# Gate and up products of a SwiGLU feed-forward with still weights: three 256 wide matmuls become one of 512 and one of 256, and their halves are added when they are read

## The chip, the cores and the metric

The kernel runs on one core of a Trainium2 chip. The metric is the device time of one execution in microseconds. The kernel before takes 1019.05 us in the median of 3 runs (1018.81 to 1019.17).

## The reference

A decoder trunk of two layers over 256 tokens with model width 1024, all in float32. Every layer has a feed-forward (FFN), a token mixer (a gated recurrence in layer 1, attention in layer 2) and a second FFN, each with normalisation before and after. The change lies in the FFN, which runs four times with a hidden width of 2816:

```python
def swiglu(x, w_gate, w_up, w_down):
    return (jax.nn.silu(x @ w_gate) * (x @ w_up)) @ w_down
```

## The kernel before

**Number format.** A float32 product is made of three matmuls: every operand `a` is split into a rounded upper part `hi` and a lower part `lo = a - hi`, and `hi*hi + hi*lo + lo*hi` is summed in PSUM. The normalised input of an FFN lies transposed in one tile `xall` of [128 rows of the model width, 8 such slices `k`, 2 parts, 256 tokens], so that for each slice the upper part's 256 columns and the lower part's 256 columns stand side by side; `xhi` and `xlo` are views of it.

**Weights.** A unit is 128 x 1024 weights (512 KB). SyncE loads it into one of 5 `raw` buffers (`load_raw`, L160); ScalarE copies it to `whi` (`split`, L175) and VectorE subtracts to get `wlo` (L176). There are 9 pairs of `whi` and `wlo`, so a unit can be split up to 9 units before it is used; the split of unit i waits until unit i - 9 is used up.

**Order of the work.** TensorE's order is written out by hand: a list of items, each of which prepares one unit (`prep`) and uses it (`work`). `slot` (L359) does one item; `tick` (L84) after it starts the next split and lets deferred small work run (`defer(n, fn)` runs `fn` n ticks later). The order on ScalarE, VectorE and GpSimd is set by the framework's scheduler, and each of these engines works its list strictly in order.

**An FFN** (`ffn_items`, L479, and `run_ffn`, L606). The hidden width is cut into five tiles of 512 and one of 256.
- In three of the four FFNs tile 0 is computed with the inputs as stationary operand and the weights moving (`proj_items`, `mm3`, L183 to L185); its hidden rows are then transposed (`hidden_T`, L506).
- All other tiles keep the weights still: a 128 x 128 block of weights is the stationary operand, and the inputs of all 256 tokens move past it (`mmj`, L195). Each call issues three matmuls of 256 columns: `whi` with `xhi` (L198), `whi` with `xlo` (L199), `wlo` with `xhi` (L200), all into the same 256 columns. I call 32 calls of `mmj` (8 slices `k` by 4 blocks of weights) a *block*: each tile of 512 is a gate block and then an up block (`tile_items`, L535); the tile of 256 is one block with gate and up in halves (`last_items`, L558). There are 38 blocks, 9 in each of three FFNs and 11 in the one where all tiles are of this kind: 1216 calls. The blocks of an FFN are counted from 1: in the first FFN, block 1 is gate and block 2 up of tile 1, block 3 and 4 those of tile 2, and so on.
- A block accumulates in two banks of PSUM, two products of 256 columns in each. When it ends, `gate_rows` (L518) runs for each bank: VectorE multiplies by the tokens' norms (L521), ScalarE takes the silu (L523). `up_rows` (L525) multiplies up by gate on VectorE (L528), and splits the product into `hhi` (ScalarE, L532) and `hlo` (VectorE, L533), the operands of the down projection.
- The down projection is `row_items` (L440): hidden rows stationary, weights moving, 512 columns per matmul, `mm3` again.

**PSUM** has 8 banks of 512 columns: 4 named `mm` for accumulation, 2 named `gt` and 2 named `tr` for transposes and other small products (L62 to L69). Each name is a ring; the framework makes a writer wait until the bank's former readers are done.

**Small work inside the blocks.** In the first FFN, `rg_params` (L670) transposes the parameters of the recurrence on TensorE (L672) some 40 ticks in, into a `tr` bank.

Of the kernel before, what the change touches and what calls it, by code (L numbers as in the profile page):

```python
# [9 lines left out]
F32 = mybir.dt.float32  # L10
# [34 lines left out]
def trunk_kernel(ctx: ExitStack, tc: tile.TileContext, A: dict, out: bass.AP):  # L45
# [15 lines left out]

    def mmbank():  # L62
        return psum.tile([P, 512], F32, tag="mm", name=nm("mm"), bufs=4)

    def gtbank():
        return psum.tile([P, 512], F32, tag="gt", name=nm("gt"), bufs=2)

    def trbank():
        return psum.tile([P, 512], F32, tag="tr", name=nm("tr"), bufs=2)  # L69
# [125 lines left out]
    def mmj(ps, wh, wl, k, first, last):  # L195

        tensor_work(3 * S)
        nc.tensor.matmul(ps, wh, xhi[:, k, :], start=first, stop=False)  # L198
        nc.tensor.matmul(ps, wh, xlo[:, k, :], start=False, stop=False)  # L199
        nc.tensor.matmul(ps, wl, xhi[:, k, :], start=False, stop=last)  # L200
# [55 lines left out]
    def rstd_rows():  # L256

        tp = trbank()
# [124 lines left out]
    def proj_items(w, c0, nn, get_x, post, nk=8):  # L383
# [4 lines left out]
        for k0 in range(0, nk, kper):  # L388
# [8 lines left out]
            def work(t, u, k0=k0, kn=kn, i=len(items)):  # L397
                if k0 == 0:
                    acc[t] = mmbank()
                ps = acc[t][:, :nn]  # L400
                if i < 2:
                    for m in range(3):
                        for j in range(kn):
                            nc.tensor.matmul(ps, get_x(t, k0 + j)[m == 2], [u.hi, u.lo, u.hi][m][:, j * nn:(j + 1) * nn],
                                             start=k0 + j + m == 0, stop=False)
                    return
                for j in range(kn):
                    k = k0 + j
                    mm3(ps, *get_x(t, k), u.hi[:, j * nn:(j + 1) * nn], u.lo[:, j * nn:(j + 1) * nn], k == 0, k == nk - 1)
                if k0 + kn == nk:  # L410
                    post(t, acc[t][:, :nn])
            if not items:
# [27 lines left out]
    def row_items(w, widths, get_x, post, rows=2):  # L440
# [6 lines left out]
        for k, kp in enumerate(widths):  # L447
# [3 lines left out]
            def work(t, u, k=k):  # L451
# [13 lines left out]
                if k == nk - 1:  # L465
                    post(t, acc[t])
            items.append((prep, work))
# [11 lines left out]
    def ffn_items(pool_of, wg, wu, wd, post_g, next_dests, last=False, normed=False, lead=1):  # L479
# [10 lines left out]
        def gate_tile():  # L490
            return pool_of().tile([P, 512], F32, tag="sil", name=nm("sil"), bufs=2)

        def prod_tile():
            return pool_of().tile([P, 8 * HA], F32, tag="prod", name=nm("prod"), bufs=2)[:, :512]

        def post_gate(t, ps):
            s = sil[t] = gate_tile()
            nc.scalar.activation(s, ps, AF.Silu, scale=rs[t][:, 0:1])

        def post_up(c0):  # L500
            def f(t, ps):
                pr = prod_tile()
# [3 lines left out]
            def hidden_T(pr, t):  # L506
                hh, hl = hid_tiles()
                tp = trbank()
# [9 lines left out]
        def gate_rows(n, ps):  # L518
            s = sil["j", n] = gate_tile()
            v = s.rearrange("p (a b) -> p a b", a=2)  # L520
            nc.vector.tensor_tensor(v, ps.rearrange("p (a b) -> p a b", a=2),  # L521
                                    rcp["v"].unsqueeze(1).to_broadcast([P, 2, S]), ALU.mult)
            nc.scalar.activation(s, s, AF.Silu)  # L523

        def up_rows(n, ps, k0):  # L525
            hh, hl = hid_tiles()
            pr = prod_tile()
            nc.vector.tensor_tensor(pr, ps, sil["j", n], ALU.mult)  # L528
            pv = pr.rearrange("p (a t b) -> p a t b", a=2, t=2)
            hv = hh[:, :, k0:k0 + 2, :].rearrange("p t a b -> p a t b")  # L530
            lv = hl[:, :, k0:k0 + 2, :].rearrange("p t a b -> p a t b")
# [3 lines left out]
        def tile_items(w, c0, post):  # L535
            acc = {}

            for k0 in range(0, 8, 2):
# [4 lines left out]
                def work(t, u, k0=k0):  # L543
                    if k0 == 0:
                        acc["b"] = [mmbank(), mmbank()]
                    for j in range(2):
                        for b in range(4):
                            o = j * 512 + b * P
                            mmj(acc["b"][b // 2][:, (b % 2) * S:(b % 2 + 1) * S], u.hi[:, o:o + P], u.lo[:, o:o + P],
                                k0 + j, k0 + j + b % 2 == 0, k0 + j == 7 and b % 2 == 1)  # L550
                        if j == 0:
                            tick()
                    if k0 == 6:
                        for n in range(2):
                            post(n, acc["b"][n])
                items.append((prep, work))

        def last_items(c0):  # L558
            acc = {}

            for k0 in range(0, 8, 2):
# [7 lines left out]
                def work(t, u, k0=k0):  # L569
                    if k0 == 0:  # L570
                        acc["b"] = [mmbank(), mmbank()]
                    for j in range(2):
                        for b in range(4):
                            o = j * 512 + b * P
                            mmj(acc["b"][b // 2][:, (b % 2) * S:(b % 2 + 1) * S], u.hi[:, o:o + P], u.lo[:, o:o + P],
                                k0 + j, k0 + j + b % 2 == 0, k0 + j == 7 and b % 2 == 1)
                        if j == 0:
                            tick()
                    if k0 == 6:
                        gate_rows(0, acc["b"][0])  # L580
                        up_rows(0, acc["b"][1], c0 // P)
# [3 lines left out]
        for i in range(5):  # L585
# [84 lines left out]
    def rg_params():  # L670
        tp = trbank()
# [34 lines left out]
    def add_gate_unit(g, k0, kn):  # L706
# [5 lines left out]
        def work(t, u):  # L712
# [6 lines left out]
            if k0 + kn == 8:  # L719
                if (g, t) not in ((0, 1), (2, 0)):  # L720
                    for gg, tt_ in {(1, 1): [(0, 1)], (2, 1): [(2, 0)]}.get((g, t), []) + [(g, t)]:
                        n = GCOLS[gg][1]
                        tok = toks[(gg, tt_)] = pools["r"].tile([P, 4 * RT], F32, tag="tok", name=nm("tok"), bufs=4)
                        nc.scalar.activation(tok[:, :n], gacc[(gg, tt_)][:, :n], AF.Gelu_apprx_tanh)
        rg[f"g{sum(n[0] == 'g' and n[1] != 'w' for n in rg)}"] = len(items)
# [36 lines left out]
    def conv(p, ps):  # L762
# [9 lines left out]
        def taps(j, i):  # L772
            for k in (2, 1, 0):
                s = 3 - k
                nc.vector.scalar_tensor_tensor(xc[:w, j, s:], ps[:w, j * S:(j + 1) * S - s],
                                               par[:w, k * NRT + i:k * NRT + i + 1], xc[:w, j, s:], ALU.mult, ALU.add)

# [80 lines left out]
    def batch(g):  # L858
# [20 lines left out]
        def gate_T(t):  # L879
            tok = toks[(g, t)]  # L880
            tp = tps[t] = trbank()
# [4 lines left out]
        def product(t):  # L886
# [4 lines left out]
            for (a, b, w) in parts_of(g):  # L891
                tp = tps[t][:w, a * P:b * P].rearrange("p (a b) -> p a b", a=b - a)
                nc.vector.tensor_tensor(y[:w, a:b, :], tp, tt[g][:w, a:b, t * P:(t + 1) * P], ALU.mult)
                nc.scalar.activation(yy[g][0][:w, t, a:b, :], y[:w, a:b, :], AF.Copy)

# [83 lines left out]
    def heads_T(pool, ps, t, n, scale, cols, dst):  # L979

        tok = pool.tile([P, 8, HA], F32, tag="prod", name=nm("htok"), bufs=2)
# [8 lines left out]
        def turn(b):  # L990
            tp = trbank()
# [42 lines left out]
    def v_items(c0, n, extra):  # L1034
# [3 lines left out]
        for k0 in range(0, 8, 2):  # L1038
# [9 lines left out]
            def work(t, u, k0=k0):  # L1048
# [6 lines left out]
                if k0 == 6:  # L1055
                    if extra:
                        post_f(t, ps[:, n:])
                    nc.scalar.activation(kv["v"][t][:, c0:c0 + n], ps[:, :n], AF.Copy, scale=rs[t][:, 0:1])
            items.append((prep, work))
# [21 lines left out]
    def attention(t):  # L1081
# [32 lines left out]
        def values(hg):  # L1114
# [8 lines left out]
            if hds[-1] % 8 == 7:  # L1123
# [3 lines left out]
                                        sm.unsqueeze(2).to_broadcast([P, 8, HD]), ALU.mult)  # L1127

# [199 lines left out]
```

## Time and profile before

| | |
|---|---|
| median of 3 runs | 1019.05 us |
| the profiled execution | 1018.94 us |
| its span, first to last instruction | 1017.2 us |
| granted TensorE clock over the span | 0.998 |
| calls of `mmj`, matmuls in them | 1216, 3648 of 6518 |
| moved by DMA | 179.07 MB, mean 176 GB/s |
| stretches in which `mmj` runs | 35.8 to 140.4, 340.0 to 444.2, 555.4 to 683.1, 846.4 to 950.6 us |

How to read it: in the profile PE is TensorE's matmuls, PEld its loads of the stationary operand, DVE is VectorE, ACT ScalarE, POOL GpSimd, SP SyncE (DMA issue). A row of a group gives the line, the engine, the operation, output and inputs by their names, the count, the busy time in us, the mean duration of one in ns, and after the second bar the engine's idle time before these instructions with what ended it. A row of the timeline gives the start and the duration in us and then the same. Matmuls are pipelined: the next one starts before the last one's row ends.

### The profile page before, as it was taken

How to read it: one execution, taken by the hardware profiler on the slowest of the kernel's cores; microseconds unless marked ns; L12 is line 12 of the kernel's file. 1: busy time of each engine (PE TensorE's matmuls, PEld its weight loads, DVE VectorE, ACT ScalarE, POOL GpSimd, SP SyncE). 2: the span in 40 equal slices, each digit the busy share in tenths (PEclk: the TensorE clock that was granted, in tenths of full speed). 3: DMA queues.
4: the chain of work that ended last, by engine and by line, in shares of the span. 5: the costliest groups of instructions: out<-in, count | busy, mean ns of one | idle time of the engine just before them, and what ended most of it. 6: DMA issues, size and time to landing. Idle time of an engine off the chain costs nothing.

```text
span 1017.2 us, 16436 instructions
## 1 busy us (share of the span) xinstructions
PE 1004.2 (99%) x6518; PEld 915.0 (90%) x6518; DVE 628.3 (62%) x777; ACT 533.9 (52%) x734; POOL 52.7 (5%) x113
## 2 busy tenths in 40 slices
PE   8999999999999999999999999999999999999997
PEld 5999998889988999998898999998888889999885
DVE  5866554668997655554695555654477476556442
ACT  5645434559986544443565444443467565444331
POOL 2500000000003000000110000000020010000000
PEclk9999999999999999999999999999999999999999
DMA  6886646565336766556376666664555067665441
GB/s 231 284 257 198 192 160 187 164 183 151 122 99 226 229 186 186 187 151 180 116 242 221 191 181 180 185 183 164 165 167 166 1 189 247 186 183 182 155 125 41
DMA packets 91875, 179.07 MB, mean 176 GB/s; under 512 B 11790, under 2 KB 31318, under 8 KB 91798
## 3 DMA queue, kind: packets, MB, share of 16 engines
q1 hardware_dynamic: 90550, 176.89, 56.1%
q8 instruction: 51, 0.84, 0.3%
q10 hardware_dynamic: 608, 1.06, 0.3%
q0 software_dynamic: 640, 0.07, 0.1%
q14 instruction: 26, 0.21, 0.1%
HBM read 176.95 MB, written 1.05 MB: 175 GB/s over the span
## 4 chain that ended last, share of the span: by engine, by line
PE 90%; ACT 4%; DVE 4%; issue 2%; POOL 1%; DVEq 0%; POOLq 0%; ACTq 0%
PE mm L198 14%; PE mm L200 14%; PE mm L199 14%; PE mm L185 13%; PE mm L184 13%; PE mm L183 13%; PE gt L815 1%; DVE wlo L176 1%; PE mm L190 1%; PE mm L191 1%; PE mm L192 1%; PE gt L1094 1%; PE mm L1121 1%; ACT junk L213 1%; PE gt L222 1%
## 5 line engine op out<-in xcount | busy, mean ns | idle before, releaser
L176 DVE TENSOR_TENSOR wlo<-raw,whi 128x1024 fp32r<-128x1024 f32 (+4 forms) x329 | 395.1, 1207 | 297.2 <-ACT whi L175 295.4
L175 ACT ACTIVATE whi<-raw 128x1024 fp32r<-128x1024 f32 (+4 forms) x329 | 342.6, 1046 | 373.8 <-PE mm L199 207.9
L198 PE MATMUL mm<-xall,whi 128*128 128x256 f32 x1216 | 344.7, 283 | 0.0
L200 PE MATMUL mm<-xall,wlo 128*128 128x256 f32 x1216 | 344.1, 283 | 0.0
L199 PE MATMUL mm<-xall,whi 128*128 128x256 f32 x1216 | 344.1, 283 | 0.0
L198 PEld LDWEIGHTS mm<-xall,whi 128*128 128x128 f32 x1216 | 233.4, 192 | 0.2
L199 PEld LDWEIGHTS mm<-xall,whi 128*128 128x128 f32 x1216 | 233.4, 192 | 0.2
L200 PEld LDWEIGHTS mm<-xall,wlo 128*128 128x128 f32 x1216 | 233.4, 192 | 0.0
L183 PE MATMUL mm<-whi,hhi 128*128 128x512 f32 (+2 forms) x432 | 166.1, 384 | 0.0
L185 PE MATMUL mm<-whi,hlo 128*128 128x512 f32 (+2 forms) x432 | 165.0, 382 | 0.0
L184 PE MATMUL mm<-wlo,hhi 128*128 128x512 f32 (+2 forms) x432 | 164.9, 382 | 0.0
L185 PEld LDWEIGHTS mm<-whi,hlo 128*128 128x128 f32 x432 | 81.1, 188 | 15.0
L184 PEld LDWEIGHTS mm<-wlo,hhi 128*128 128x128 f32 x432 | 81.2, 188 | 14.7
L183 PEld LDWEIGHTS mm<-whi,hhi 128*128 128x128 f32 x432 | 81.2, 188 | 14.6
L183 PE MATMUL mm<-whi,xall 128*128 128x512 f32 (+2 forms) x168 | 67.1, 400 | 0.1
L184 PE MATMUL mm<-wlo,xall 128*128 128x512 f32 (+2 forms) x168 | 65.0, 387 | 0.4 <-DVE wlo L1191 0.2
L185 PE MATMUL mm<-whi,xall 128*128 128x512 f32 (+2 forms) x168 | 64.8, 386 | 0.1
L206 POOL TENSOR_SCALAR nv<-ss 128x1 f32<-128x1 f32 x24 | 10.9, 453 | 789.7 <-ACT junk L213 789.5
L184 PEld LDWEIGHTS mm<-wlo,xall 128*128 128x128 f32 x168 | 31.7, 188 | 7.4 <-DVE wlo L176 1.2
L185 PEld LDWEIGHTS mm<-whi,xall 128*128 128x128 f32 x168 | 31.6, 188 | 7.0 <-DVE xall L236 1.1
L183 PEld LDWEIGHTS mm<-whi,xall 128*128 128x128 f32 x168 | 31.6, 188 | 5.7 <-ACT xall L231 0.5
L277 DVE SCALAR_TENSOR_TENSOR t<-mm,rstd,gb 128x512 f32<-128x512 f32 x16 | 11.9, 749 | 26.7 <-ACT junk L213 26.7
(188 smaller groups left out, 938.9 us busy)
## 6 DMA issues: line engine op xcount, KB each, us to landing
raw<-in_ffn_w_down_dram SPq DMA_DIRECT2D x88, 512.0 KB
raw<-in_ffn_w_up_dram SPq DMA_DIRECT2D x80, 512.0 KB
raw<-in_ffn_w_gate_dram SPq DMA_DIRECT2D x79, 512.0 KB
raw<-in_rg_w_in_dram SPq DMA_DIRECT2D x20, 504.0 KB
raw<-in_rg_w_out_dram SPq DMA_DIRECT2D x10, 504.0 KB
raw<-in_ffn_w_gate_dram SPq DMA_DIRECT2D x18, 256.0 KB
raw<-in_ffn_w_up_dram SPq DMA_DIRECT2D x16, 256.0 KB
raw<-in_w_kv_dram SPq DMA_DIRECT2D x8, 512.0 KB
```

The costliest lines, as they stand in the source:

```text
L175: nc.scalar.activation(hi[:parts, c:c + m], rawv[:, c:c + m], AF.Copy)
L176: nc.vector.tensor_tensor(lo[:parts, c:c + m], rawv[:, c:c + m], hi[:parts, c:c + m].bitcast(F32), ALU.subtract)
L183: nc.tensor.matmul(ps, xh, wh, start=first, stop=False)
L184: nc.tensor.matmul(ps, xh, wl, start=False, stop=False)
L185: nc.tensor.matmul(ps, xl, wh, start=False, stop=last)
L190: nc.tensor.matmul(ps, wh, xh, start=first, stop=False)
L191: nc.tensor.matmul(ps, wh, xl, start=False, stop=False)
L198: nc.tensor.matmul(ps, wh, xhi[:, k, :], start=first, stop=False)
L199: nc.tensor.matmul(ps, wh, xlo[:, k, :], start=False, stop=False)
L200: nc.tensor.matmul(ps, wl, xhi[:, k, :], start=False, stop=last)
L206: nc.gpsimd.tensor_scalar(v, ss[:, 0:1], ss[:, 1:2] if n == 2 else 0.0, D * EPS * f * f, ALU.add, ALU.add)
L277: nc.vector.scalar_tensor_tensor(t1[n], pf[n], r_in, gb[:, n * 512:(n + 1) * 512], ALU.mult, ALU.mult)
```

## The change

Three things change together.

1. `mmj` issues two matmuls. The upper and lower input parts, side by side in `xall`, pass `whi` as one product of 512 columns that fills a whole bank: the left 256 columns take `whi*xhi`, the right 256 take `whi*xlo`. The second matmul adds `wlo*xhi` to the left 256.
2. A block therefore takes four whole banks. PSUM becomes one tile `pall` of 8 banks that the kernel hands out itself (`bank`, `release`): gate blocks take banks 4 to 7, which are those of `gt` and `tr`, up blocks banks 0 to 3, those of `mm`; the last block takes 4 to 7. While a block holds its banks, small transposes go to the other set (`sparebank`).
3. Left and right halves are added when the block is read (`total`): ScalarE copies the right halves of all four banks to SBUF, VectorE adds the left halves. The multiplication by the norms (gate) or by the gate (up) then works on SBUF. The steps that took two passes of 512 columns take one of 1024; the two tiles of 512 for `sil` and for `prod` become one of 1024.

The core of the diff:

```diff
+    pall = psum.tile([P, 8, 512], F32, name="pall")
+    lent = set()
+    order = {"mm": [0, 1, 2, 3], "gt": [4, 5], "tr": [6, 7]}
+    held = {}
+
+    def bank(kind, hold=False):
+
+        i = next(i for i in order[kind] if i not in held)
+        assert i not in lent, (kind, i)
+        order[kind].remove(i)
+        order[kind].append(i)
+        b = pall[:, i, :]
+        if hold:
+            held[i] = b
+        return b
...
+    def sparebank():
+        return bank("mm" if 6 in lent else "tr")
...
-    def mmj(ps, wh, wl, k, first, last):
+    def mmj(b, wh, wl, k):
 
         tensor_work(3 * S)
-        nc.tensor.matmul(ps, wh, xhi[:, k, :], start=first, stop=False)
-        nc.tensor.matmul(ps, wh, xlo[:, k, :], start=False, stop=False)
-        nc.tensor.matmul(ps, wl, xhi[:, k, :], start=False, stop=last)
+        nc.tensor.matmul(pall[:, b, :], wh, xall[:, k, :, :].rearrange("p a b -> p (a b)"), start=k == 0, stop=False)
+        nc.tensor.matmul(pall[:, b, :S], wl, xhi[:, k, :], start=False, stop=k == 7)
...
-        def gate_rows(n, ps):
-            s = sil["j", n] = gate_tile()
-            v = s.rearrange("p (a b) -> p a b", a=2)
-            nc.vector.tensor_tensor(v, ps.rearrange("p (a b) -> p a b", a=2),
-                                    rcp["v"].unsqueeze(1).to_broadcast([P, 2, S]), ALU.mult)
+        def total(v, b, m):
+
+            nc.scalar.activation(v, pall[:, b:b + m, S:], AF.Copy)
+            nc.vector.tensor_tensor(v, pall[:, b:b + m, :S], v, ALU.add)
+
+        def gate_rows(b, m):
+            s = sil["j"] = gate_tile(m * S)
+            v = s.rearrange("p (a b) -> p a b", a=m)
+            total(v, b, m)
+            nc.vector.tensor_tensor(v, v, rcp["v"].unsqueeze(1).to_broadcast([P, m, S]), ALU.mult)
             nc.scalar.activation(s, s, AF.Silu)
 
-        def up_rows(n, ps, k0):
+        def up_rows(b, m, k0):
             hh, hl = hid_tiles()
-            pr = prod_tile()
-            nc.vector.tensor_tensor(pr, ps, sil["j", n], ALU.mult)
-            pv = pr.rearrange("p (a t b) -> p a t b", a=2, t=2)
...
+            pr = prod_tile(m * S)
+            total(pr.rearrange("p (a b) -> p a b", a=m), b, m)
+            nc.vector.tensor_tensor(pr, pr, sil["j"], ALU.mult)
+            pv = pr.rearrange("p (a t b) -> p a t b", a=m, t=2)
...
+        def still(t, u, k0, b0):
+            if k0 == 0:
+                assert not set(held) & set(range(b0, b0 + 4)), held.keys()
+                lent.update(range(b0, b0 + 4))
+            for j in range(2):
+                for b in range(4):
+                    o = j * 512 + b * P
+                    mmj(b0 + b, u.hi[:, o:o + P], u.lo[:, o:o + P], k0 + j)
+                if j == 0:
+                    tick()
+            if k0 == 6:
+                lent.difference_update(range(b0, b0 + 4))
...
-                tile_items(wg, i * 512, gate_rows)
-                tile_items(wu, i * 512, lambda n, ps, i=i: up_rows(n, ps, 4 * i + 2 * n))
+                tile_items(wg, i * 512, 4, gate_rows)
+                tile_items(wu, i * 512, 0, lambda b, m, i=i: up_rows(b, m, 4 * i))
...
     def rg_params():
-        tp = trbank()
+        tp = sparebank()
```

`rstd_rows`, `gains_T`, `hidden_T` and `heads_T` take `sparebank` in place of `trbank` in the same way, and the readers of the `mm` banks call `release` when they have been issued.

More of the change, by code (lines that the diff above doesn't have):

```diff
@@ L411, in work @@
                     post(t, acc[t][:, :nn])
+                    release(acc[t])
             if not items:
@@ L569, in work @@
                 def work(t, u, k0=k0):
[L570 to L578, printed above, removed]
+                    still(t, u, k0, 4)
                     if k0 == 6:
-                        gate_rows(0, acc["b"][0])
-                        up_rows(0, acc["b"][1], c0 // P)
+                        gate_rows(4, 2)
+                        up_rows(6, 2, c0 // P)
                 items.append((prep, work))
```

70 lines of the change are left out of this document (38 added, 32 removed).

## The prediction

> **What bounds the kernel now.** I read the page from the top: the engines' busy time, the granted clock, the chain that ended last, the costliest groups.
>
> ```profile
> span 1017.2 us, 16436 instructions
> ## 1 busy us (share of the span) xinstructions
> PE 1004.2 (99%) x6518; PEld 915.0 (90%) x6518; DVE 628.3 (62%) x777; ACT 533.9 (52%) x734; POOL 52.7 (5%) x113
> ...
> PEclk9999999999999999999999999999999999999999
> ...
> PE 90%; ACT 4%; DVE 4%; issue 2%; POOL 1%; DVEq 0%; POOLq 0%; ACTq 0%
> PE mm L198 14%; PE mm L200 14%; PE mm L199 14%; PE mm L185 13%; PE mm L184 13%; PE mm L183 13%; PE gt L815 1%; DVE wlo L176 1%; PE mm L190 1%; PE mm L191 1%; PE mm L192 1%; PE gt L1094 1%; PE mm L1121 1%; ACT junk L213 1%; PE gt L222 1%
> ...
> L176 DVE TENSOR_TENSOR wlo<-raw,whi 128x1024 fp32r<-128x1024 f32 (+4 forms) x329 | 395.1, 1207 | 297.2 <-ACT whi L175 295.4
> L175 ACT ACTIVATE whi<-raw 128x1024 fp32r<-128x1024 f32 (+4 forms) x329 | 342.6, 1046 | 373.8 <-PE mm L199 207.9
> L198 PE MATMUL mm<-xall,whi 128*128 128x256 f32 x1216 | 344.7, 283 | 0.0
> L200 PE MATMUL mm<-xall,wlo 128*128 128x256 f32 x1216 | 344.1, 283 | 0.0
> L199 PE MATMUL mm<-xall,whi 128*128 128x256 f32 x1216 | 344.1, 283 | 0.0
> ```
>
> PE is busy 99% of the span, at full clock, and 90% of the chain runs through it. The three matmuls of `mmj` (L198 to L200) carry 42% of that chain and never wait (idle 0.0). The split on ACT (L175) stands idle mainly until PE frees a weight buffer: the weights are ahead, and PE is what the rest waits for.
>
> Matmuls overlap, so the 283 ns of a row are no price. The price is the distance from start to start, read in the timeline. First the matmuls of `mmj`, 256 wide, then those of the down projection, 512 wide:
>
> ```profile
> 80.16 0.28 PE L198 MATMUL mm<-xall,whi 128*128 128x256 f32 x1
> ...
> 82.68 0.28 PE L198 MATMUL mm<-xall,whi 128*128 128x256 f32 x1
> ```
>
> ```profile
> 700.05 0.39 PE L183 MATMUL mm<-whi,hhi 128*128 128x512 f32 x1
> ...
> 702.77 0.39 PE L183 MATMUL mm<-whi,hhi 128*128 128x512 f32 x1
> ```
>
> The first stretch is 7 groups of three: 2.52 / 21 = 0.1200 us for each 256 wide matmul. The second is 4 groups of three: 2.72 / 12 = 0.2267 us for each 512 wide one. Twice the width costs 0.0133 us less than two matmuls; in a straight line through both points, about 0.0133 us of every matmul does not depend on its width. The change lives on that part.
>
> How full the other engines are where `mmj` runs is seen in a table of the four stretches (columns: length, busy time of PE, PEld, DVE, ACT and POOL with instruction counts, clock, DMA share, GB/s):
>
> ```profile
> 35.80:140.40 104.60, 104.60 (x872) 104.40 (x871) 67.71 (x88) 52.32 (x60) 3.91 (x6) 1.00 0.70 219
> 340.00:444.20 104.20, 104.20 (x870) 104.16 (x870) 62.15 (x65) 46.96 (x53) 0.11 (x1) 1.00 0.64 197
> 555.40:683.10 127.70, 127.70 (x1066) 127.66 (x1066) 74.86 (x77) 58.12 (x66) 0.00 (x0) 1.00 0.63 188
> 846.40:950.60 104.20, 104.20 (x870) 104.16 (x870) 62.15 (x65) 46.97 (x53) 0.00 (x0) 1.00 0.64 197
> ```
>
> Together 440.7 us, in which DVE works 266.9 and ACT 204.4.
>
> **The change part by part.**
>
> *The merged product.* Each of 1216 calls of `mmj` now issues one 512 wide and one 256 wide matmul in place of three 256 wide ones. Before: 3 x 0.1200 = 0.3600 us. After, if each costs what it costs among its own kind: 0.2267 + 0.1200 = 0.3467 us. Saved 0.0133 x 1216 = **16.2 us**. What the trace lacks is a run in which the two widths alternate. It has single changes of width:
>
> ```profile
> 555.22 0.39 PE L185 MATMUL mm<-whi,hlo 128*128 128x512 f32 x1
> 555.45 0.28 PE L198 MATMUL mm<-xall,whi 128*128 128x256 f32 x1
> 555.57 0.28 PE L199 MATMUL mm<-xall,whi 128*128 128x256 f32 x1
> ```
>
> ```profile
> 222.70 0.28 PE L192 MATMUL mm<-xall,wlo 128*126 128x256 f32 x1
> 222.81 0.39 PE L183 MATMUL mm<-whi,xall 128*128 128x504 f32 x1
> 223.04 0.39 PE L184 MATMUL mm<-wlo,xall 128*128 128x504 f32 x1
> ```
>
> Wide to narrow takes 0.23 and then 0.12, narrow to wide 0.11 and then 0.23. Nothing extra is paid at the seam; the load of the next weights is hidden in both directions. Bounds: with 0.230 for the wide one (these rows) 0.0100 x 1216 = 12.2 us are saved; with 0.110 for the narrow one 0.0233 x 1216 = 28.3 us. I take 16.2, from the two long stretches, since single rows are rounded to 0.01 us. A third of the weight loads goes too; they are hidden, so nothing is booked.
>
> *The sums at the read.* The two halves of a bank must be added. Per block (32 calls of `mmj`, before 11.52 us, after 32 x 0.3467 = 11.09 us) ACT copies the right halves and DVE adds the left ones; then DVE multiplies from SBUF. I price this from the ACT and the DVE rows of the stretch in which block 4 of the first FFN (an up block) ended:
>
> ```profile
> 82.81 1.06 ACT L175 ACTIVATE whi<-raw 128x1024 fp32r<-128x1024 f32 x1 [1.82 <-PE mm L199]
> 83.78 1.14 ACT L532 ACTIVATE hhi<-prod 128x512 fp32r<-128x512 f32 x2
> ```
>
> ```profile
> 82.16 1.41 DVE L528 TENSOR_TENSOR prod<-mm,sil 128x512 f32<-128x512 f32 x2
> 83.90 1.23 DVE L176 TENSOR_TENSOR wlo<-raw,whi 128x1024 fp32r<-128x1024 f32 x1 [0.33 <-ACT whi L175]
> 85.05 1.29 DVE L533 TENSOR_TENSOR hlo<-prod,hhi 128x512 fp32r<-128x512 f32 x2
> ```
>
> A 1024 wide ACT pass is 1.06 us (L175), two 512 wide ones 1.14 (L532). A 1024 wide DVE pass is 1.23 us from SBUF (L176), two 512 wide ones from PSUM 1.41 (L528); I take 1.3 for the add. A full block gains one ACT copy less 0.08 of merging, 0.98 us, and on DVE an add and a multiply in place of two multiplies, 1.3 + 1.23 - 1.41 = 1.12 us. For 34 full and 4 half-drained blocks that is some 37 us on ACT and 40 us on DVE, spread over 441 - 16 = 425 us: ACT (204 + 37) / 425 = 57%, DVE (267 + 40) / 425 = 72%. Neither becomes the bound. The cover is PE's own 11.09 us per block. If it went, the price would be the drain itself (next part).
>
> *The banks.* A block now takes four banks instead of two, and gate blocks lie in the banks of `gt` and `tr`; the next gate block needs them again one whole up block (11.09 us) later. The drain after a block's end: where a split stands ahead of the copy on ACT, 0.97 (L175, next ACT start at 83.78) + 1.06 copy + 1.3 add = 3.4 us; without it 2.4 us. Up to 7.7 us are left, so PE does not wait at block starts: **nothing**. At the step from the last block (banks 4 to 7) to the down projection (banks 0 to 3) the same 11.09 us lie between.
>
> *What is moved into a bank just filled.* While a gate block runs, the small transposes go to banks 0 to 3, those of the up block that just ended. I went through PE's order of the changed program for such places: the transposes of the hidden rows and of the gains take banks read long before; one does not. The transpose of the recurrent parameters (L672), issued four `mmj` after block 4, takes bank 2 and so must wait for the add:
>
> ```profile
> 82.56 0.28 PE L200 MATMUL mm<-xall,wlo 128*128 128x256 f32 x1
> ...
> 84.12 0.24 PE L672 MATMUL tr<-ident,prow 88*126 88x88 f32 x1
> ```
>
> The block ends with the matmul of 82.56, which releases ACT at 82.81. In the built program ACT's next is a split (that of row 82.81), then the copy: 83.78 to 84.8. DVE's next is that split's low part, 83.90 to 85.05, then the add to 85.05 + 1.3 = 86.35. PE would be at the transpose at 82.68 + 4 x 0.3467 = 84.07. It stands **2.3 us**, and behind it in order stands every later matmul. Bounds: 1.1 us if the copy went first (82.81 + 1.06 + 1.3 = 85.2); 3.5 if one more DVE split came before.
>
> *Nothing else.* SP's loads keep their order and count. A unit of 512 KB is used in 8 x 0.3467 = 2.77 us: 189 GB/s against 182 before, where the first stretch above moved 219. POOL is untouched. The `release` bookkeeping issues nothing. Outside the gate and up blocks PE's order is the same, instruction by instruction.
>
> *Sum*, against the profiled execution's own 1018.94 us (span 1017.2 and 1.7 around it; the median of the runs is 1019.05, 0.1 above): 1018.94 - 16.2 + 2.3 = **1005.0 us**.
>
> **The rivals.**
>
> *The drain becomes the bound (slower).* Place: the first matmul of each block, which waits for the add of the block two before. It costs nothing until the drain exceeds 11.09 us, and turns the change into a loss when it exceeds that by 16.2 / 37 = 0.44 us. A split on ACT waits for PE to free a buffer, one each 2.77 us; with three of them ahead of the copy the drain is 3.4 + 3 x 2.77 = 11.7 us and PE stands 37 x 0.6 = 22 us: 1027. For it: ACT works strictly in order and L175 waits for PE for 207.9 us. Against it: at most one split stands ahead of the copy in the built program, and the engines are at 57 and 72%. Chance 0.05.
>
> *The fixed part does not go with the matmul (no change, just slower).* The third matmul's 0.0133 us may be hidden in the streak of narrow ones and come back at each change of width: 0.24 + 0.12 = 0.36 us per call. Then only the new wait is left: 1018.9 + 2.3 = 1021.2; with a fifth of the gain, 3.2 us, 1018.0. For it: no row alternates. Against it: both seams above. The Trainium skill (TensorE: Matmul & The Clock Gate, section Back-to-back issue gap) gives the gap of an isolated matmul as width / 2.4 + 2.5 ns, so 109.2 and 215.8 ns; by that only 2.5 ns per call would go, an estimate by that page of 3.0 us in all. By that page's rule the two long stretches above would be shorter; they show 120.0 and 226.7 ns, and the trace decides. Chance 0.05.
>
> *Part of the gain is given back in small waits (faster, by less).* 0.2 us at each of 38 block starts, from the additional semaphores and late drains: 7.6 us, 1012.6. For it: the trace has no block of this form. Against it: the 7.7 us of slack. Chance 0.07.
>
> **How the numbers follow.** Forecast 0.83. Its own range: 1018.94 - 12.2 + 3.5 = 1010.2 at the slow end; at the fast end 28.3 is no serious gain since it rests on one rounded seam, so I let the narrow matmul come down to 0.118: 0.0153 x 1216 = 18.6, with 1.1 of waiting, 1001.4. The range for 8 in 10 is 1001.4 to 1010.2. A measurement of this kernel tells about 0.2% (2 us) from no change. Faster: 0.83 + 0.07 = 0.90. Of the second rival's 0.05 I count 0.03 within 0.2% and 0.02 beyond it: same 0.03, slower 0.05 + 0.02 = 0.07.
>
> **What would show it.** Right: the wide matmul followed by the narrow one 0.227 later and the next wide one 0.120 after that, a full block 11.1 us long, the four stretches together about 424.5 us plus the wait; one hole of about 2 us on PE before the parameters' transpose in the first FFN, released by DVE's add, and none at block starts; DVE near 72% in the stretches. Wrong: a pair nearer to 0.36 us (the second rival), PE rows at block starts released by the add (the first or third), or splits on ACT that wait for DMA rather than PE, which would mean that the faster pace outran the weights.

## The result, and the profile after

The changed kernel takes 1008.23 us in the median of three executions (1007.29, 1008.23, 1009.17); a fourth took 4195 us, for a reason not known, and is left out (with it the median is 1008.7). The kernel before takes 1019.11 us (1018.81 to 1019.47). The ratio is 0.9893, with a 95% interval of 0.9874 to 0.9913. The forecast was 1005.0 us with a range of 1001.4 to 1010.2, so the change is faster, inside the range, and its gain is 3.2 us short of the forecast. The profiled execution took 1007.29 us (span 1005.6).

The page of the changed kernel, in the parts that answer to those shown of before (L222 is the wide matmul of `mmj`, L223 the narrow one, L199 the split on ACT):

```profile
span 1005.6 us, 13910 instructions
## 1 busy us (share of the span) xinstructions
PE 991.0 (99%) x5302; PEld 847.3 (84%) x5302; DVE 665.3 (66%) x768; ACT 566.1 (56%) x742; POOL 51.5 (5%) x113
...
PEclk9999999999999999999999999999999999999999
...
PE 70%; issue 21%; ACT 4%; DVE 4%; POOL 1%; DMA 0%; DVEq 0%; POOLq 0%; ACTq 0%
...
L199 ACT ACTIVATE whi<-raw 128x1024 fp32r<-128x1024 f32 (+4 forms) x329 | 342.1, 1044 | 290.3 <-PE pall L209 125.6
L222 PE MATMUL pall<-xall,whi 128*128 128x512 f32 x1216 | 424.7, 395 | 0.0
L223 PE MATMUL pall<-xall,wlo 128*128 128x256 f32 x1216 | 338.4, 278 | 0.0
```

1216 matmuls are gone (6518 to 5302). PE is still busy 99%, neither line of `mmj` has any idle time before it, and the split still idles mainly for PE, not for DMA (asked for L199 alone, the profile has PE end 230 of its 290 us of idle time, DMA some 8): the faster pace did not outrun the weights. The chain's share of PE has fallen from 90 to 70% and that of "issue" has risen from 2 to 21%. Most of it is no wait: 171 us are one piece from 822.0 us on, and from there to 993.0 us PE has no idle time. DVE and ACT rose by 37.0 and 32.2 us of busy time, against 40 and 37 forecast.

The four stretches of `mmj` (length, then busy time of PE, PEld, DVE, ACT and POOL, clock, DMA share, GB/s):

```profile
36.00:139.50 103.50, 101.37 (x586) 88.49 (x585) 75.49 (x84) 59.75 (x62) 4.12 (x6) 1.00 0.70 222
338.80:441.30 102.50, 102.50 (x583) 88.96 (x583) 69.19 (x61) 54.31 (x55) 0.00 (x0) 1.00 0.65 199
552.20:675.50 123.30, 123.30 (x715) 107.89 (x714) 83.68 (x72) 67.09 (x68) 0.00 (x0) 1.00 0.65 195
838.60:939.20 100.60, 100.60 (x583) 87.98 (x582) 69.14 (x60) 54.28 (x55) 0.00 (x0) 1.00 0.66 203
sum 429.90, PE 427.77 PEld 373.32 DVE 297.50 ACT 235.44 POOL 4.12; mean PE 106.94 PEld 93.33 DVE 74.37 ACT 58.86 POOL 1.03
```

The sum line is the one to compare with 440.7 of before; its windows end a little later behind the last matmul, so the fairer measure is from the first to the last start of `mmj` in each stretch, together 439.9 us before and 428.1 us now. The lines show two things. DVE is at 297.5 / 429.9 = 69% and ACT at 55%; no engine became the bound. And in the first stretch, and only there, PE is less busy than the stretch is long, by 2.1 us. Now compare the second row with the fourth: the same work (9 blocks), no idle time in either, and yet 1.9 us between them. Before, these two stretches were both 104.2 us. That difference is most of what the forecast missed.

**The wait.** The timeline of PE, ACT and DVE around the parameters' transpose (L699) in the changed kernel:

```profile
82.41 1.00 ACT L549 ACTIVATE prod<-pall 128x1024 f32<-128x1024 f32 x1
82.54 1.22 DVE L200 TENSOR_TENSOR wlo<-raw,whi 128x1024 fp32r<-128x1024 f32 x1 [1.55 <-ACT whi L199]
82.58 0.28 PE L223 MATMUL pall<-xall,wlo 128*128 128x256 f32 x1
83.68 1.22 DVE L550 TENSOR_TENSOR prod<-pall,prod 128x1024 f32<-128x1024 f32 x1
...
85.00 0.27 PE L699 MATMUL pall<-ident,prow 88*126 88x88 f32 x1 [2.13 <-issue]
```

PE issues nothing between 82.58 and 85.00, 2.42 us where 0.12 is normal: 2.3 us lost. The view calls the releaser "issue", but the rows name it: the add of the right and left halves (L550) ends at 83.68 + 1.22 = 84.90, and the transpose into that bank starts 0.10 later. Ahead of the add stands the split's low part, as in the built order. The waits of PE name no other line of the change:

```profile
engine line waited for: us in total, times, longest us
PE pall L699 <- issue: 2.1, 1, 2.1
PE pall L151 <- DVE idle L137: 1.5, 1, 1.5
PE pall L340 <- DVE hn L333: 0.8, 2, 0.4
```

**Two cadences.** Eight calls of `mmj` (one unit of weights) are the grain in which the pace shows. In the third FFN, two rows 40 units apart, then in the second FFN two rows 30 units apart:

```profile
558.72 0.39 PE L222 MATMUL pall<-xall,whi 128*128 128x512 f32 x1
...
669.66 0.39 PE L222 MATMUL pall<-xall,whi 128*128 128x512 f32 x1
```

```profile
350.57 0.40 PE L222 MATMUL pall<-xall,whi 128*128 128x512 f32 x1
...
435.37 0.40 PE L222 MATMUL pall<-xall,whi 128*128 128x512 f32 x1
```

110.94 / 40 = 2.773 us a unit, which is 0.3467 a call, the forecast to the last digit; and 84.80 / 30 = 2.827, 0.3533 a call. Both hold without a break through their stretch. A *cadence* is what I call such a steady spacing. By the trace's starts in nanoseconds the first repeats every two calls (wide to narrow 231 and 233, narrow to wide 112 and 118), the second every three (241, 236, 233 and 120, 113, 117). Before, all units took 2.880. So half of the merged matmul's gain (0.0067 of 0.0133 us a call) is lost wherever the second cadence rules, 0.054 us a unit.

### The profile page after: what moved, and what is told of

Same layout as the page of the kernel before. It is cut to its first block, busy times and chain, and to the rows that moved or that the text cites. A ratio compares the mean times of both kernels' runs of the same rounds, so it can differ in the third digit from the quotient of the medians.

```text
span 1005.6 us, 13910 instructions
## 1 busy us (share of the span) xinstructions
PE 991.0 (99%) x5302; PEld 847.3 (84%) x5302; DVE 665.3 (66%) x768; ACT 566.1 (56%) x742; POOL 51.5 (5%) x113
## 3 DMA queue, kind: packets, MB, share of 16 engines
q10 hardware_dynamic: 608, 1.06, 0.3%
## 4 chain that ended last, share of the span: by engine, by line
PE 70%; issue 21%; ACT 4%; DVE 4%; POOL 1%; DMA 0%; DVEq 0%; POOLq 0%; ACTq 0%
PE pall L222 21%; PE pall L223 11%; PE pall L209 10%; PE pall L208 10%; PE pall L207 10%; PE pall L845 1%; DVE wlo L200 1%; PE pall L214 1%; PE pall L215 1%; PE pall L216 1%; PE pall L1128 1%; ACT junk L236 1%; PE pall L1155 1%; ACT whi L199 1%; PE pall L1026 1%
## 5 line engine op out<-in xcount | busy, mean ns | idle before, releaser
L199 ACT ACTIVATE whi<-raw 128x1024 fp32r<-128x1024 f32 (+4 forms) x329 | 342.1, 1044 | 290.3 <-PE pall L209 125.6
L222 PE MATMUL pall<-xall,whi 128*128 128x512 f32 x1216 | 424.7, 395 | 0.0
L223 PE MATMUL pall<-xall,wlo 128*128 128x256 f32 x1216 | 338.4, 278 | 0.0
L222 PEld LDWEIGHTS pall<-xall,whi 128*128 128x128 f32 x1216 | 228.1, 188 | 53.3
L223 PEld LDWEIGHTS pall<-xall,wlo 128*128 128x128 f32 x1216 | 228.8, 188 | 0.2
L207 PE MATMUL pall<-whi,hhi 128*128 128x512 f32 (+2 forms) x432 | 166.0, 384 | 0.0
L209 PE MATMUL pall<-whi,hlo 128*128 128x512 f32 (+2 forms) x432 | 165.0, 382 | 0.0
L208 PE MATMUL pall<-wlo,hhi 128*128 128x512 f32 (+2 forms) x432 | 164.8, 382 | 0.0
L208 PEld LDWEIGHTS pall<-wlo,hhi 128*128 128x128 f32 x432 | 81.2, 188 | 14.7
L207 PEld LDWEIGHTS pall<-whi,hhi 128*128 128x128 f32 x432 | 81.2, 188 | 14.6
L207 PE MATMUL pall<-whi,xall 128*128 128x512 f32 (+2 forms) x168 | 67.1, 400 | 0.1
L209 PE MATMUL pall<-whi,xall 128*128 128x512 f32 (+2 forms) x168 | 64.9, 386 | 0.1
```

The lines of the kernel that those rows point to most:

```text
L199: nc.scalar.activation(hi[:parts, c:c + m], rawv[:, c:c + m], AF.Copy)
L207: nc.tensor.matmul(ps, xh, wh, start=first, stop=False)
L208: nc.tensor.matmul(ps, xh, wl, start=False, stop=False)
L209: nc.tensor.matmul(ps, xl, wh, start=False, stop=last)
L222: nc.tensor.matmul(pall[:, b, :], wh, xall[:, k, :, :].rearrange("p a b -> p (a b)"), start=k == 0, stop=False)
L223: nc.tensor.matmul(pall[:, b, :S], wl, xhi[:, k, :], start=False, stop=k == 7)
```

## The experiments

Theory: the gain is the fixed part of the matmul that is gone, the one loss is the wait at the parameters' transpose, and what else is missing is the second cadence. Rivals: the sums and the banks cost something of their own; the drain has little room; the second cadence is a matter of the wait, or of the wide matmul.

**e1: the changed kernel again**, no edit.

> The changed kernel once more, on the chip of the other runs of this group, with its own profile. In the profile of the changed kernel three of the four stretches with mmj run at 2.773 us per unit of 8 calls (0.3467 per call, the forecast), and the second, from 344.9 us on, at 2.827 (0.3533), 34 units x 0.054 = 1.8 us more. Theory A (the cadence is set by how the stream of matmuls starts up in a stretch, not by this stretch's work): another stretch, or none, or several, run at 2.827 this time, and the time lies between 1005.0 (none) and 1012.5 (all four: 2 x 1.9 and 2.3 more than 1007.3 in all 1007.3 + 34x0.054 + 42x0.054 + 34x0.054 = 1013.2). Theory B (something in the second FFN slows it): again the second stretch, and only that, and 1007.3.

1008.12 us (1007.86 to 1009.56), ratio 0.989 [0.9873, 0.9906]. In its profile the second FFN has 2.827 again, but so has the first up to the parameters' transpose (the table behind e10), so neither theory of the expectation fits. The profiled execution is the longest of these, 1009.56, and shows a further loss. The granted clock in the windows behind the wait:

```profile
82.60:86.20 3.60, 1.48 (x10) 1.10 (x9) 3.04 (x3) 1.40 (x2) 0.00 (x0) 1.00 0.64 164
86.20:89.40 3.20, 3.20 (x12) 2.70 (x11) 2.41 (x5) 2.61 (x4) 0.00 (x0) 0.50 0.60 185
89.40:92.60 3.20, 3.20 (x19) 2.78 (x19) 1.94 (x8) 2.12 (x3) 0.00 (x0) 0.96 0.40 84
```

Behind the wait the clock is 0.50 for 3.2 us. PE is busy all that time, but 12 matmuls pass where 19 pass in the next 3.2 us. The same place in the timeline:

```profile
87.22 0.63 PE L222 MATMUL pall<-xall,whi 128*128 128x512 f32 x1
87.65 0.42 PE L223 MATMUL pall<-xall,wlo 128*128 128x256 f32 x1
87.86 0.63 PE L222 MATMUL pall<-xall,whi 128*128 128x512 f32 x1
```

Wide 0.43 and narrow 0.21 us. A call takes 0.64 instead of 0.3467, so of the 3.2 us a part of 3.2 x (1 - 0.3467 / 0.64) = 1.5 us is lost. The profile first shown has the same wait (2.3 us) and no such drop, as its row behind the wait says:

```profile
85.00:88.20 3.20, 3.20 (x19) 2.80 (x20) 2.41 (x4) 2.01 (x3) 0.00 (x0) 1.00 0.68 199
```

The Trainium skill (TensorE: Matmul & The Clock Gate, section What's actually happening) has the gate halve PE's clock after an idle window of some 3.4 us, and lets these windows run free of the kernel. That one of two executions is hit, and for 3.2 us and a little more (0.96 in the next row), agrees with it. That the wait must fill a window does not: it lasted 2.4 us, and in the 3.60 us of the first row PE was busy for 1.48.

**e2: the transpose three ticks later.**

```diff
-    defer(40, rg_params)
+    defer(43, rg_params)
```

> The transpose of the recurrent parameters is issued 3 ticks (12 calls of mmj, 4.2 us) later, 5.5 us after its block's end; everything else is as in the changed kernel. My theory (the transpose waits for VectorE's add on bank 2, 2.3 us of PE): the gap of 2.41 us ahead of this transpose shrinks to about 0.12, no new gap appears, and the time falls by 2.3 us against the changed kernel in the same cadence. Rival (PE would have stood anyway, for the parameters' DMA or a later bank): the gap stays or moves, and the time is the same.

1005.75 us (1005.65 to 1006.72), ratio 0.9869 [0.9855, 0.9884]: 2.4 us less than e1. The transpose now stands in the stream without a hole:

```profile
87.49 0.28 PE L223 MATMUL pall<-xall,wlo 128*128 128x256 f32 x1
87.61 0.24 PE L699 MATMUL pall<-ident,prow 88*126 88x88 f32 x1
87.64 0.48 PE L222 MATMUL pall<-xall,whi 128*128 128x512 f32 x1
```

The wait was the bank's, and its price is what the rows gave. The profiled execution, 1006.72 us, is the longest of the four; in it the first FFN goes over to 2.827 behind the transpose and stays there for its last 17 units or so, 17 x 0.054 = 0.9 us (the table behind e10). Which cadence the other three had is not known. No other version has a lower median, though those of e9 and e10 are too close to be told apart from it.

**e3: the wide matmul as two of 256 columns**, into the same bank's halves; sums, banks and wait stay.

```diff
-        nc.tensor.matmul(pall[:, b, :], wh, xall[:, k, :, :].rearrange("p a b -> p (a b)"), start=k == 0, stop=False)
+        nc.tensor.matmul(pall[:, b, :S], wh, xhi[:, k, :], start=k == 0, stop=False)
+        nc.tensor.matmul(pall[:, b, S:], wh, xlo[:, k, :], start=False, stop=False)
```

> The product of 512 columns is taken apart again into two of 256, into the left and the right half of the same bank; banks, sums at the read and all else stay as in the changed kernel. My theory (the whole gain is the fixed part of one matmul per call): 0.360 us per call again, the stretches together as long as before plus the one wait of 2.3 us: 1018.9 + 2.3 = 1021.2 us. Rival (part of the gain, or a hidden loss, comes from the banks or the sums): the time differs from 1021.2 by that part; at 1019 the wait would not be lost time, above 1023 the sums and banks would cost more than the one wait.

1021.99 us (1021.24 to 1023.53), ratio 1.0028 [1.0018, 1.0038]. Two rows of the second FFN, 30 units apart, and the wait of the transpose (here L700):

```profile
354.41 0.28 PE L222 MATMUL pall<-xall,whi 128*128 128x256 f32 x1
...
440.81 0.28 PE L222 MATMUL pall<-xall,whi 128*128 128x256 f32 x1
```

```profile
PE pall L700 <- issue: 2.1, 1, 2.1
```

86.40 / 30 = 2.880 a unit, as before the change, and the wait. Without the merged matmul the change is a loss of its wait: the whole gain is the fixed part, and the sums and the banks cost nothing else. The profiled execution, 1021.24 us, is what was expected (1021.2); the median is 0.8 us above that. The mean granted clock of the eight executions suggests why: four with 0.999 took 1021.24 to 1021.49 us, three with 0.996 took 1022.49 to 1023.53, one with 0.998 took 1023.05. There is no second cadence here, and 0.996 to 0.997 is what e1 and e7 show with their stretch of half clock (all profiles without one have 0.998 or 0.999). So half the clock seems to follow the wait in some of these executions too; no profile of them was kept.

**e4: four wide, then four narrow matmuls** for each slice `k`, the same matmuls in another order.

```diff
                 for b in range(4):
                     o = j * 512 + b * P
-                    mmj(b0 + b, u.hi[:, o:o + P], u.lo[:, o:o + P], k0 + j)
+                    mmw(b0 + b, u.hi[:, o:o + P], k0 + j)
+                for b in range(4):
+                    o = j * 512 + b * P
+                    mmn(b0 + b, u.lo[:, o:o + P], k0 + j)
```

> The order inside a slice k: first the four wide products of the four blocks of weights, then their four narrow ones, in place of wide and narrow in turn. If the price of a matmul is its own fixed part and width, 4 x 0.2267 + 4 x 0.1200 = 1.387 us per slice, 2.773 per unit: the same as the changed kernel in its faster cadence. If the slower cadence of 2.827 comes from the alternation of widths, it is not seen here in any stretch, and the time is 1005.4 or a little less (1007.3 less 1.9); if it comes from how a stretch starts, some stretch may show it here too. Against both: if a change of width costs something by itself, with a quarter of the changes this order is faster than 2.773.

1009.98 us (1009.67 to 1010.18), ratio 0.9908 [0.9894, 0.9923]. I had expected the faster cadence or less everywhere; that failed. The second FFN, 30 units apart:

```profile
351.78 1.09 PE L222 MATMUL pall<-xall,whi 128*128 128x512 f32 x4
...
435.78 0.39 PE L222 MATMUL pall<-xall,whi 128*128 128x512 f32 x1
```

84.00 / 30 = 2.800 here, and 2.807 in the other three FFNs. So with a quarter of the changes of width the surplus over 2.773 is there in all four FFNs. It is no price per change of width: the faster cadence has 16 changes a unit and none of it.

**e5: e2, and every sum done twice**, to see how much room the drain has.

```diff
-            nc.scalar.activation(v, pall[:, b:b + m, S:], AF.Copy)
-            nc.vector.tensor_tensor(v, pall[:, b:b + m, :S], v, ALU.add)
+            for _ in range(2):
+                nc.scalar.activation(v, pall[:, b:b + m, S:], AF.Copy)
+                nc.vector.tensor_tensor(v, pall[:, b:b + m, :S], v, ALU.add)
```

> The run with the later parameters' transpose, with the sums at the read done twice over (copy, add, copy, add; the second pass writes the same values). The drain of a block grows by about 1.06 + 1.3 = 2.4 us, from 3.4 to 5.8 us, and ACT and VectorE carry some 38 x 1.06 and 38 x 1.3 us more. My theory (7.7 us of slack before a bank is needed again): no wait at any block start, the time stays at that of the later transpose, 1005.7 us, within 0.2%. Rival (the drains already cost something at the block starts): PE waits for the add at the blocks' starts, and the time rises by up to 37 x 2.4 = 89 us, or by a good part of it.

1006.65 us (1005.77 to 1008.01), ratio 0.9879 [0.9864, 0.9894]. The first two stretches, and the one wait of PE that e2 does not have:

```profile
36.00:139.50 103.50, 102.80 (x592) 89.70 (x591) 84.68 (x93) 68.33 (x72) 3.87 (x6) 1.00 0.69 223
338.80:441.30 102.50, 102.50 (x582) 88.91 (x581) 77.98 (x67) 62.38 (x64) 0.00 (x0) 1.00 0.64 196
```

```profile
PE pall L700 <- issue: 0.7, 1, 0.7
```

DVE is at 82 and 76% of these stretches and still no block start waits. Only the parameters' transpose, moved just far enough in e2, is again too early, by 0.7 us. The median is 0.9 us above that of e2, which ran on another chip, so the drain doubled costs about that wait.

**e6 and e7: e2, and the hidden rows' transposes one or two ticks later** in the three FFNs that have them (three and four ticks after tile 0's product), to see whether the place of an interruption decides the cadence.

```diff
-HT = 2
+HT = 3
```

> Later parameters' transpose, and the transposes of the hidden rows in the first, second and fourth FFN 3 instead of 2 ticks after their product: they interrupt the stream of mmj 4 calls later. Theory A (the cadence of mmj, 0.3467 or 0.3533 us per call, is chosen anew at each interruption and then kept): at least one of these three FFNs changes its cadence against the run with the later transpose alone, where the first had 0.3467 up to the parameters' transpose and 0.3533 after it, the second 0.3533, the third and fourth 0.3467; the third, which is not touched, keeps 0.3467. With the second at 0.3467 the time falls by 1.9 us, to about 1003.8; with the fourth at 0.3533 it rises by as much. Theory B (the cadence belongs to the place in the program, its data or addresses): second FFN 0.3533 and fourth 0.3467 as before, time 1005.7.

> The same with 4 ticks, so 8 calls later than in the changed kernel. Theory A: again some of the three FFNs change, independently of the run with 3 ticks; time between 1003.8 (second FFN at 0.3467, nothing lost elsewhere) and 1007.6. Theory B: as with the later transpose alone, 1005.7.

e6: 1006.70 us (1006.36 to 1007.19), ratio 0.988 [0.9863, 0.9896]. e7: 1010.16 us (1009.71 to 1013.10), ratio 0.9918 [0.9903, 0.9933], above the 1007.6 at which the expectation ended, with a wait of a new kind. The first of the waits of PE in e7, and the clock behind it:

```profile
PE pall L222 <- DVE hlo L544: 2.6, 1, 2.6
```

```profile
37.00:41.00 4.00, 1.41 (x8) 1.01 (x7) 4.00 (x5) 3.44 (x4) 4.00 (x6) 0.98 0.85 286
41.00:44.00 3.00, 3.00 (x11) 2.52 (x11) 2.72 (x3) 1.14 (x2) 0.64 (x2) 0.50 0.92 335
```

Four ticks after the product, the transposes fall into a bank that the gate block needs next, and the first matmul into that bank, in the block's third call (L222), waits 2.6 us for their reader (L544), again with 3 us at half the clock behind it. It is a wait at a block start, as the prediction feared of the sums, but not from the sums; two ticks keep clear of it. As to the cadence (table below): the second FFN stays at 2.827 in both runs, the fourth goes over to 2.827 in e7 alone, and the first comes out the other way round in e6. The first differs between executions anyway, so only the fourth speaks for the place, with one profile.

**e8: e2, and the narrow matmul made 512 wide too**, so that `wlo` also meets the lower half, one execution.

```diff
-        nc.tensor.matmul(pall[:, b, :S], wl, xhi[:, k, :], start=False, stop=k == 7)
+        nc.tensor.matmul(pall[:, b, :], wl, xall[:, k, :, :].rearrange("p a b -> p (a b)"), start=False, stop=k == 7)
```

> The narrow product is made 512 wide too: the lower weights pass both input parts, so the product of the two lower parts, which the kernel otherwise leaves out, is added into the right half. The stream of mmj then has one width. This measures a 512 wide matmul among its own kind in this very stream. If it costs 0.2267 us as in the down projection, a call takes 0.4533, a unit 3.627, there is no second cadence, and the time is 1005.7 - (part of the slower cadence, 2 to 3) + 1216 x 0.1067 = 1133; then the slower cadence belongs to the mixture of widths. If it costs 0.231 to 0.236, as in the order four and four, a call takes 0.462 to 0.472, and the surplus belongs to the wide matmul with these operands, not to the mixture: 1144 to 1156 us.

1133.32 us. The second FFN, 30 units apart:

```profile
382.72 0.39 PE L222 MATMUL pall<-xall,whi 128*128 128x512 f32 x1
...
491.52 0.39 PE L222 MATMUL pall<-xall,whi 128*128 128x512 f32 x1
```

108.80 / 30 = 3.627, twice 0.2267 a call, and so in all FFNs. With e3 (2.880 throughout): streams of one width have one pace, whichever the width. So the second cadence belongs to the mixture, as far as one profile of each can say.

**e9 and e10: the second FFN alone, interrupted elsewhere.** e9 is e2 with one 88x88 transpose that nobody reads, in block 3, the second gate block (`nudge`, a new argument of `ffn_items`, is set for the second FFN alone):

```diff
                     still(t, u, k0, b0)
+                    if nudge and c0 == 1024 and b0 == 4 and k0 == 4:
+                        nc.tensor.transpose(sparebank()[:88, :88], ident[:88, :88], ident[:88, :88])
```

e10 is e2 with the hidden rows' transposes five ticks after their block (`ht`, a new argument of `ffn_items` that takes the place of `HT`) in that FFN only:

```diff
-    ffn_b = ffn_items(lambda: pools["f"], A["ffn2_w_gate"][0], A["ffn2_w_up"][0], A["ffn2_w_down"][0], A["ffn2_post_g"][0], dests_l1)
+    ffn_b = ffn_items(lambda: pools["f"], A["ffn2_w_gate"][0], A["ffn2_w_up"][0], A["ffn2_w_down"][0], A["ffn2_post_g"][0], dests_l1, ht=5)
```

> The later parameters (1005.75), and one 88x88 transpose that nobody reads, put into the third gate block of the second FFN, 4 calls-of-eight before the block's end. The second FFN ran at 2.827 us per 8 calls in every profile so far. Theory A (the cadence is taken up anew at every interruption of the alternating stream, as behind the parameters' transpose in the first FFN, where it changed in four of five profiles): behind the new transpose the second FFN goes on at 2.773, which over the 25 units left is 25 x 0.054 = 1.35 us less, minus some 0.1 for the transpose: 1004.5. Theory B (something in the second FFN itself, its tiles or its buffers, sets 2.827): the units behind it stay at 2.827 and the time is 1005.9.

> The later parameters (1005.75), and in the second FFN alone the hidden rows' transposes 5 instead of 2 ticks after their block, so that they interrupt the alternating stream at another place. Theory A: the cadence of the second FFN is chosen at those transposes; if it comes out as 2.773, the 34 units cost 1.9 us less, 1003.9; if it comes out as 2.827 again, 1005.8. Theory B (the second FFN's own tiles set it): 2.827 and 1005.8. A wait of some 2.6 us at the gate block's start, as the transposes 4 ticks later brought to the first FFN, would show as a gap before L222 and give 1008 to 1010.

e9: 1006.13 us (1005.73 to 1007.13), ratio 0.9872 [0.9856, 0.9889]. e10: 1005.92 us (1005.57 to 1006.33), ratio 0.9872 [0.9857, 0.9886]. The second FFN behind the idle transpose (L592) of e9, 24 units, and that of e10, 30 units:

```profile
370.02 0.24 PE L592 MATMUL pall<-ident 88*88 88x88 f32 x1
370.05 0.48 PE L222 MATMUL pall<-xall,whi 128*128 128x512 f32 x1
...
437.96 0.40 PE L222 MATMUL pall<-xall,whi 128*128 128x512 f32 x1
```

```profile
349.45 0.40 PE L222 MATMUL pall<-xall,whi 128*128 128x512 f32 x1
...
434.25 0.40 PE L222 MATMUL pall<-xall,whi 128*128 128x512 f32 x1
```

67.91 / 24 = 2.830 and 84.80 / 30 = 2.827: the second FFN keeps its slower cadence through both. The theory that an interruption changes the cadence finds no support in this FFN; that it is drawn anew and comes out the same is not excluded by two profiles. All profiles with the new `mmj` order together, us a unit:

| profile | FFN 1, up to the parameters' transpose | FFN 1, behind it | FFN 2 | FFN 3 | FFN 4 |
|---|---|---|---|---|---|
| after | 2.773 | 2.773 | 2.827 | 2.773 | 2.773 |
| e1 | 2.827 | 2.773 | 2.827 | 2.773 | 2.773 |
| e2 | 2.773 | 2.827 | 2.827 | 2.773 | 2.773 |
| e5 | 2.773 | 2.773 | 2.827 | 2.773 | 2.773 |
| e6 | 2.827 | 2.773 | 2.827 | 2.773 | 2.773 |
| e7 | 2.773 | 2.827 | 2.827 | 2.773 | 2.827 |
| e9 | 2.773 | 2.827 | 2.827 | 2.773 | 2.773 |
| e10 | 2.827 | 2.773 | 2.827 | 2.773 | 2.773 |

After and e1 are one program and begin the first FFN differently. So do e9 and e10, which have the same code up to the second FFN and ran on one chip: there the cadence differs from execution to execution. At the parameters' transpose it changed in six of eight: where the transpose had to wait (after, e1, e5) the cadence behind it was 2.773 each time, and where it did not (the other five) it went over to the other one each time. The idle transpose of e9 did not wait either and changed nothing. The second and third FFN came out the same way eight times. A cadence never changed except where other instructions stood between the calls.

## Why the prediction came out as it did

- *The merged product*, 16.2 us: the mechanism was right, the size was not. e3 shows that it alone is the gain. The value per call was exact in the first, third and fourth FFN of this profile (0.3467). It was 0.3533 in the second, 34 units x 0.054 = 1.9 us short. This is the term that was mis-sized: from the first to the last start of each stretch the four gained 14.0 us beside the wait, of 16.2 forecast. The step that failed is "Nothing extra is paid at the seam": it was read from single changes of width, rounded to 0.01 us, and a pattern that only a long mixture has can't show there. The lower bound taken, 12.2 us, did cover it.
- *The sums at the read*: right. No wait at a block start, ACT 55% and DVE 69% where 57 and 72 were forecast; the copy took 1.00 and the add 1.22 us (L549, L550) against 1.06 and 1.3. e5 shows room for a second drain.
- *The banks*: right, no wait in any stretch.
- *What is moved into a bank just filled*: right in place, cause and size, 2.3 us. All events came 1.4 us earlier than in the working, so the difference held. e2 shows the cause. What was not foreseen is what can follow: 3.2 us at half the clock and 1.5 us more, in e1.
- *Nothing else*: right as far as the profiles reach; splits still wait for PE and not for DMA.
- *The sum* for the profiled execution: 1018.94 - 14.0 + 2.3 = 1007.2, and it took 1007.29. The other two executions, 1008.23 and 1009.17, lie 0.9 and 1.9 us above that. The first FFN in its slower cadence (up to 36 x 0.054 = 1.9 us) and the half clock (1.5 us) are of that size, and e1's profile has some of both. The mean granted clock of the longest is 0.996, which points to the half clock; the cadence of executions without a profile can't be read.
- *Two slips of the working* change nothing: 0.97 + 1.06 + 1.3 is 3.3 us and not 3.4, and the row of 82.81 names L199 as what released ACT, not the block's last matmul.
- *The rivals*: that the drain becomes the bound falls by the stretches of the changed kernel, without a wait at any block start, and by e5. That the fixed part does not go with the matmul falls by the two rows of the third FFN; in the second FFN half of it is true, in a way that the rival did not describe (a slower pattern, not a price at each change of width, see e4). The Trainium skill's fixed part (TensorE: Matmul & The Clock Gate, section Back-to-back issue gap), 2.5 ns, would have given some 3 us, an estimate by that page; the runs show 14.0. Small waits at block starts were not seen in the changed kernel.

**Open:** what sets the cadence. The slower one is there without the wait (e2, e9), is not the wide matmul's own (e8), does not grow with the number of width changes (e4), and in the second FFN gave way neither to one more interruption (e9) nor to another place of the hidden transposes (e6, e7, e10). Where the operands of each FFN lie in SBUF, and how the start of the stream falls against the load of the weights, were not tried.

## What to carry to other kernels

Where PE bounds a kernel and matmuls are narrow, merging two that share their weights is worth up to the fixed part of one, here 13.3 ns each and half of that in the slower cadence, if the additional sums fit beside PE; price it from the distance between starts, and measure the mixture of widths itself before trusting it. When a ring of banks becomes shared, go through PE's order for every small product that lands in a bank just filled: a single one cost 2.3 us here, three ticks of delay removed it, and behind a wait of that length the clock may halve.

## What the hardware showed that I had not expected

- A stream that alternates 512 and 256 wide matmuls has two stable paces, 0.3467 and 0.3533 us a pair, and kept one, in all eight profiles, for as long as nothing else came between; four wide and four narrow in turn take 0.3500 to 0.3509 a pair. Streams of one width took 0.1200 or 0.2267 each in every stretch measured (before, e3, e8).
- After PE stood for 2.4 us (e1) or 2.6 us (e7) the granted clock was 0.50 for about 3 us, but not in every execution (not in the first profile, after 2.4 us). By the starts in nanoseconds the spacings there are 427 and 213, two to one, so that at this clock no fixed part of a matmul is left to see.
